# Three-pass products for the block-diagonal gates and the attention-weighted sums of a two-block transformer kernel

## The chip, the cores and the metric

The kernel runs on one core of one Trainium2 chip, as one program. A core has TensorE (PE, the matmul array), VectorE (DVE), ScalarE (ACT), GpSimd (POOL), a queue that issues loads (SyncE, SP), the on-chip memory SBUF (128 partitions) and PSUM, into which TensorE writes its products. The metric is device time in microseconds for one execution; the time of a kernel is the median of its runs.

## What is computed

A sequence of 512 tokens of width 1024 in float32 passes a first block (which this change does not touch) and then two equal layers of a second block. Cut to what matters, a layer is:

```
x = x + 0.5 * swiglu(rms_norm(x, ffn1_norm), w_gate, w_up, w_down)      # width 2816
h = rms_norm(x, mix_norm)
q, k, v, f_logit, xr, gr, g_attn, g_rnn = split(h @ w_in + b_in)
q, k = rms_norm per head; 8 heads of 128
y_attn = forgetting_attention(q, k, v, log_sigmoid(f_logit)) @ w_o_attn
xr = causal_depthwise_conv(xr)                                          # 4 taps
yr = rg_lru(xr) * gelu(gr);  y_rnn = yr @ w_o_rnn
x = x + (sigmoid(g_attn) * y_attn + sigmoid(g_rnn) * y_rnn) @ w_out
x = x + 0.5 * swiglu(rms_norm(x, ffn2_norm), ...)

forgetting_attention, a head, a block of 128 queries:
    s = q_i @ k.T * scale + (c_i[:, None] - c[None, :])    # c = cumsum(log_f)
    p = softmax(where(causal, s, -inf));   out = p @ v
rg_lru:
    r, i = sigmoid(block_diag(x, w_a) + b_a), sigmoid(block_diag(x, w_x) + b_x)   # 16 blocks of 64 x 64
    a = exp(-8 r softplus(-lam));  h_t = a_t h_(t-1) + sqrt(1 - a_t^2) i_t x_t
```

## The kernel before, in words

Activations lie transposed in SBUF, as tiles of 128 channels by 512 tokens. Every large product is made in three passes: each factor is split into a `hi` and a `lo` half (`split`, L222; `w`, L183, for weights), and `mm3` (L228) issues hi x hi, hi x lo and lo x hi (L230, L231, L232) with fp32r operands into one accumulator. Weights come from HBM in chunks of 256 KB in a planned order; for each chunk ScalarE makes `hi` (L198), VectorE makes `lo` (L199), and a ring of four holds each of raw, hi and lo. `acc` gives the four PSUM accumulators (tag `a`); `pair` makes two output tiles of 128 channels, `tokens` makes four tiles of 128 tokens by 512 columns. Four more PSUM banks are named `xm` (1), `xh` (1) and `xs` (2).

SBUF tiles come from pools by tag, each tag with so many buffers: an allocation beyond them waits for the oldest reader to be done. Pools opened inside an `ExitStack` give their memory back at its end, and the next pool opened takes that memory. The order of the instructions on each engine is laid out when the program is built, by a scheduler that takes, of what is ready by its own clock, the earliest in the program's text first, and work under `hp()` before other work. On the chip each engine then keeps that order.

In a layer's mixer (`mix`, L966) the order in the text is: the sum of squares to a scale per token (`stats`), four pairs for `xr`, the recurrent branch (`rnn`, L899), the forget gates (L1014 to L1032, whose cumulative row goes through DRAM and comes back as `cb`, one row a head, spread over the partitions), and then twice, for four heads each (`hf` 0 and 1): tokens for q, k and v with their eviction at L1044, the normalising and transposing of q and k (`heads_T`, L379, which runs under `hp()`; four transposes at L400 through the one bank `xm`, each copied to SBUF at L402), `attn`, and two pairs for the gelu branch. Then come the two output projections with their gates, and `w_out`.

In `rnn` each of the eight channel tiles is convolved (L910, L912), and the two gates are plain f32 matmuls with 128 x 128 block-diagonal weights (L914, L915). In `attn` each head has four query blocks: `attn_scores` (L841) makes the scores and the softmax, one row of tiles `s`; `attn_values` (L861) transposes the weights block by block (L868), copies them to SBUF (L870) and multiplies v with them as plain f32 matmuls of 128 columns (L872), one block behind the scores. The sums of a head gather in `xh` and are copied to a tile `x` (L886). v has six tiles of its own, `qk` five, `cb` two, `bq` (the bias row of q, k or v) one; `keep`, which lives through the whole kernel, has `x` (8), `y` (1) and `p` (1) among others.

Of the kernel before, what the change touches and what calls it, by code (L numbers as in the profile page):

```python
# [7 lines left out]
F32 = mybir.dt.float32  # L8
F32R = mybir.dt.float32r
U8 = mybir.dt.uint8  # L10
AF = mybir.ActivationFunctionType
OP = mybir.AluOpType
# [107 lines left out]
class Build:  # L120
# [98 lines left out]
        self.tc.keep_in_program_order(ins)  # L219
        return ins  # L220

    def split(self, src, tag):  # L222
        hi, lo = self.t(tag, F32R), self.t(tag, F32R)
        self.nc.scalar.copy(hi, src)
        self.nc.vector.tensor_tensor(lo, src, hi.bitcast(F32), op=OP.subtract)
        return hi, lo
# [631 lines left out]
        nc.vector.tensor_scalar(s, s, ri, None, op0=OP.mult)  # L858
        return st

    def attn_values(self, st, v, vc, i, o):  # L861

        nc = self.nc
        n = (i + 1) * 128
        pt = self.aux("xs")
        for j in range(i + 1):
            js = slice(j * 128, j * 128 + 128)
            nc.tensor.transpose(pt[:, js], st[:, js], self.ident)  # L868
        pT = self.t("pT")
        nc.scalar.copy(pT[:, :n], pt[:, :n])  # L870
        for j in range(i + 1):
            nc.tensor.matmul(o[:, i * 128:n], v[j][:, vc:vc + 128], pT[:, j * 128:j * 128 + 128],  # L872
                             start=(i == 0 and j == 0), stop=(i == 3 and j == 3), skip_group_check=True)

    def attn(self, qT, kT, v, hd0, ct, cdram):

        nc = self.nc
        out, todo = [], []

        def values(st, hd, i):  # L880
            if i == 0:
                out.append(self.aux("xh"))
            self.attn_values(st, v, (hd - hd0) * 128, i, out[-1])
            if i == 3:
                y = self.t("x")
                nc.scalar.copy(y, out[-1])  # L886
                out[-1] = y

        for hd in range(hd0, hd0 + 4):
            cb = self.t("cb")  # L890
            nc.gpsimd.dma_start(cb, cdram[hd:hd + 1, :].to_broadcast([128, 512]))
            for i in range(4):
                todo.append((self.attn_scores(qT[hd - hd0], kT[hd - hd0], i, hd, ct, cb), hd, i))
                if len(todo) > 1:
                    values(*todo.pop(0))
        values(*todo.pop(0))
        return out

    def rnn(self, xr, bd, l, hb, sp4):  # L899
        nc = self.nc  # L900
        hs = []
        for j0 in range(0, 8, 4):
            av, vv, ix = [], [], []
            for j in range(j0, j0 + 4):
                xc = self.t("xc")
                for tap in range(CW2):
                    wv = self.col(("conv_w_2", l), j * CW2 + tap)
                    src = xr[j][:, tap:tap + 512]
                    if tap == 0:
                        nc.vector.tensor_scalar(xc, src, wv, self.col(("conv_b_2", l), j), op0=OP.mult, op1=OP.add)  # L910
                    else:
                        nc.vector.scalar_tensor_tensor(xc, src, wv, xc, op0=OP.mult, op1=OP.add)  # L912
                ga, gx = self.aux("xs"), self.aux("xs")
                nc.tensor.matmul(ga, bd[0][j // 4][:, j % 4], xc, start=True, stop=True)  # L914
                nc.tensor.matmul(gx, bd[1][j // 4][:, j % 4], xc, start=True, stop=True)  # L915
                ti, th, a = self.t("abc"), self.t("abc"), self.t("hm")
                nc.scalar.activation(th, ga, AF.Tanh, scale=0.5, bias=hb[:, j:j + 1])
                nc.scalar.activation(ti, gx, AF.Tanh, scale=0.5, bias=hb[:, 8 + j:9 + j])
                nc.scalar.activation(a, th, AF.Exp, scale=sp4[:, 8 + j:9 + j], bias=sp4[:, 8 + j:9 + j])
                nc.scalar.activation(th, th, AF.Tanh, scale=sp4[:, j:j + 1], bias=sp4[:, j:j + 1])  # L920
                a2 = self.square(a, "xc")
                nc.vector.scalar_tensor_tensor(th, a2, 1.0, th, op0=OP.add, op1=OP.mult)
                nc.vector.scalar_tensor_tensor(ti, ti, 1.0, xc, op0=OP.add, op1=OP.mult)
                av.append(a)
                vv.append(th)
                ix.append(ti)
            for v in vv:
                self.pin(nc.scalar.activation(v, v, AF.Sqrt, scale=0.25))
            for a, v, i in zip(av, vv, ix):
                nc.vector.tensor_tensor(i, i, v, op=OP.mult)  # L930
                nc.vector.tensor_tensor_scan(a, a, i, 0.0, op0=OP.mult, op1=OP.add)
            hs += av
        return hs
# [32 lines left out]
    def mix(self, l):  # L966
        nc = self.nc
        h = self.hx
        with ExitStack() as ctx:
            lp = ctx.enter_context(self.tc.tile_pool(name=f"lp{l}", bufs=1))  # L970
            self.pool(ctx, f"mb{l}", hm=8, t=3, bq=1, qk=5, v=6, qkT=8, cb=2, s=3, pT=2)
            with self.hp():
                rt, rb = self.stats()
            hb = self.lined(lp, (128, 32), name="hb")
# [7 lines left out]
            def scaled(a, tag):  # L982
                y = self.t(tag)
                with self.hp():
                    nc.vector.tensor_tensor(y, a, rb, op=OP.mult)
                return y

            ct = self.lined(lp, (128, 32), name="ct")
            cdram = self.dp.tile([8, 512], F32, name=f"cd{l}")
            with ExitStack() as c2:  # L990
                pool = self.pool(c2, f"rn{l}", bd=4, xc=3, abc=8)
                bd = []
                for nm in ("lru_w_a_2", "lru_w_x_2"):
                    b = [self.t("bd", shape=(128, 4, 128)) for _ in range(2)]
                    for hh in range(2):
                        nc.gpsimd.memset(b[hh], 0.0)
                        src = self.ap[nm][l, hh * 8:hh * 8 + 8].rearrange("(j two) c d -> two c j d", two=2)
                        nc.gpsimd.dma_start(b[hh][0:64, :, 0:64], src[0])
                        nc.gpsimd.dma_start(b[hh][64:128, :, 64:128], src[1])
                    bd.append(b)  # L1000

                xr = []
                for m in range(0, 8, 2):
                    for a in self.pair("w_in_2", l, 8, MIX + m * 128, h):
                        y = scaled(a, "t")
                        u = self.lined(pool, (128, 512 + CW2 - 1), tag="xr", bufs=3, name=self.id("xr"))
                        nc.gpsimd.memset(u[:, :CW2 - 1], 0.0)
                        with self.hp():
                            nc.scalar.activation(u[:, CW2 - 1:], y, AF.Identity, bias=self.col(("b_mix", l), len(xr)))
                        xr.append(u)  # L1010
                hs = self.rnn(xr, bd, l, hb, sp4)
                self.tap(f"hs{l}", hs[0])

            fa = self.acc()  # L1014
            for k0 in (0, 4):
                hi, lo = self.w("w_in_2", l, k0, 4, 3072, 128)
# [14 lines left out]
                nc.tensor.transpose(ps[:, i * 8:i * 8 + 8], fc[:, i * 128:i * 128 + 128], self.ident[0:8, 0:8])  # L1031
            nc.vector.tensor_copy(ct, ps[:, 0:32])  # L1032
            self.tap(f"fc{l}", fc)
            ya = []
            for hf in range(2):
                for n in range(3):
                    bq = self.t("bq")
                    c = n * 1024 + hf * 512
                    nc.gpsimd.dma_start(bq, self.ap["brow"][l:l + 1, c:c + 512].to_broadcast([128, 512]))
                    ts = []  # L1040
                    for tt, a in enumerate(self.tokens("w_in_2", l, c, h)):
                        v = self.t("v" if n == 2 else "qk")
                        with self.hp():
                            nc.vector.scalar_tensor_tensor(v, a, rt[:, tt:tt + 1], bq, op0=OP.mult, op1=OP.add)  # L1044
                        ts.append(v)
                    if n == 0:
                        qT = self.heads_T(ts, 4, 128, qg)
                    elif n == 1:
                        kT = self.heads_T(ts, 4, 128, self.col(("k_norm_2", l)))
# [19 lines left out]
            for n, (o, wn) in enumerate(((3072, "w_o_rnn_2"), (2048, "w_o_attn_2"))):  # L1069
# [4 lines left out]
                for m in range(0, 8, 2):  # L1074
                    ga = self.pair("w_in_2", l, 8, MIX + o + m * 128, h)
                    yo = self.pair(wn, l, 8, m * 128, yh if n else yr)
                    for i in range(2):
                        with self.hp():
                            s = scaled(ga[i], "t" if n else "hm")
# [3 lines left out]
                            if n:  # L1083
                                g = mg[m + i]
# [6 lines left out]
            x = self.x  # L1091
# [100 lines left out]
```

## Time and profile before

| | us |
|---|---|
| median of 3 runs | 3413.01 (3413.0 to 3414.46) |
| the profiled execution | 3414.17 |
| its span, first to last instruction | 3412.4 |
| PE busy | 3390.8 |
| DVE busy | 1877.1 |
| ACT busy | 1307.6 |
| POOL busy | 165.0 |

The trace names an instruction by engine, line of the kernel, operation, and the tiles it writes and reads (out<-in). Matmuls are pipelined: their durations overlap, so what one of them occupies on TensorE is read from the distance between starts. A plain f32 matmul is recorded as two matmuls; a transpose, and a pass of `mm3`, as one. The records' starts just after a plain f32 matmul can lie early by the time that the matmul ahead still takes.

### The profile page before, as it was taken

To read this page: it belongs to the slowest core of one execution; us is meant where nothing else is said; L and a number is where in the kernel's file an instruction comes from. 1 tells how busy PE (TensorE), PEld (TensorE's weight loads), DVE (VectorE), ACT (ScalarE), POOL (GpSimd) and SP (SyncE) were. 2 spreads that over 40 slices of the span, in tenths; PEclk is the share of its full clock that TensorE was granted. 3 is DMA by queue.
4 is the path that set the end of the run, shared out by engine and by line. 5 is a ranking of instruction groups with operands and counts; after the bars stand their busy time and mean duration, and the time that the engine had idled before them with its cause. 6 is when DMAs were issued, how large, how long until landed. Compare 5 with 4: busy or idle time off the path is not lost.

```text
span 3412.4 us, 41999 instructions
## 1 busy us (share of the span) xinstructions
PE 3390.8 (99%) x15370; PEld 2769.3 (81%) x15370; DVE 1877.1 (55%) x3148; ACT 1307.6 (38%) x2282; POOL 165.0 (5%) x274
## 2 busy tenths in 40 slices
PE   8999999999999999999999999999999999999999
PEld 6887777888888888788888888888887788888887
DVE  7698654534444444876455444444447865454442
ACT  3335443423333333654333333333336544343331
POOL 0011100000000001111000000000010110000000
PEclk9999999999999999999999999999999999999999
DMA  6223533433333333322333333333343222333332
GB/s 217 72 76 105 155 113 108 130 98 97 96 96 96 96 117 105 90 91 89 111 97 95 99 96 97 95 99 96 102 123 95 86 89 81 123 95 98 96 104 91
DMA packets 180623, 351.33 MB, mean 103 GB/s; under 512 B 20672, under 2 KB 21952, under 8 KB 180416
## 3 DMA queue, kind: packets, MB, share of 16 engines
q1 hardware_dynamic: 174112, 329.07, 31.8%
q0 software_dynamic: 6160, 19.37, 1.8%
q8 instruction: 121, 1.98, 0.2%
q14 instruction: 86, 0.70, 0.1%
q10 hardware_dynamic: 144, 0.20, 0.0%
HBM read 342.24 MB, written 6.32 MB: 102 GB/s over the span
## 4 chain that ended last, share of the span: by engine, by line
PE 97%; DVE 2%; ACT 1%; issue 0%; DMA 0%; POOL 0%; SPq 0%; DVEq 0%; ACTq 0%
PE a L232 30%; PE a L230 30%; PE a L231 30%; PE xh L872 1%; PE xs L847 1%; PE xh L437 1%; PE xh L519 1%; PE xs L497 1%; PE xs L868 1%; PE xm L400 0%; DVE xc L912 0%; DVE lo L199 0%; PE xh L513 0%; PE xh L476 0%; PE xs L914 0%
## 5 line engine op out<-in xcount | busy, mean ns | idle before, releaser
L199 DVE TENSOR_TENSOR lo<-raw,hi 128x512 fp32r<-128x512 f32 x1144 | 784.8, 687 | 1257.1 <-ACT hi L198 1240.9
L198 ACT CAST hi<-raw 128x512 fp32r<-128x512 f32 x1144 | 707.0, 619 | 1572.2 <-PE a L231 1265.3
L231 PE MATMUL a<-h,hi 128*128 128x512 f32 x2528 | 989.4, 392 | 0.0
L230 PE MATMUL a<-h,hi 128*128 128x512 f32 x2528 | 984.7, 392 | 1.7 <-ACT h L599 1.7
L232 PE MATMUL a<-h,lo 128*128 128x512 f32 x2528 | 982.4, 392 | 0.0
L230 PEld LDWEIGHTS a<-h,hi 128*128 128x128 f32 x2528 | 475.4, 188 | 105.6 <-issue 6.1
L232 PEld LDWEIGHTS a<-h,lo 128*128 128x128 f32 x2528 | 475.1, 188 | 105.2 <-issue 7.2
L231 PEld LDWEIGHTS a<-h,hi 128*128 128x128 f32 x2528 | 475.0, 188 | 101.5 <-issue 3.6
L230 PE MATMUL a<-act,hi 128*128 128x512 f32 x960 | 373.4, 389 | 0.0
L231 PE MATMUL a<-act,hi 128*128 128x512 f32 x960 | 373.4, 389 | 0.0
L232 PE MATMUL a<-act,lo 128*128 128x512 f32 x960 | 372.8, 389 | 0.0
L231 PE MATMUL a<-Y,hi 128*128 128x512 f32 x544 | 214.5, 394 | 0.0
L230 PE MATMUL a<-Y,hi 128*128 128x512 f32 x544 | 213.7, 393 | 0.0
L232 PE MATMUL a<-Y,lo 128*128 128x512 f32 x544 | 212.8, 391 | 0.0
L232 PEld LDWEIGHTS a<-act,lo 128*128 128x128 f32 x960 | 180.2, 188 | 37.5
L230 PEld LDWEIGHTS a<-act,hi 128*128 128x128 f32 x960 | 180.2, 188 | 37.4
L231 PEld LDWEIGHTS a<-act,hi 128*128 128x128 f32 x960 | 180.2, 188 | 37.3
L232 PE MATMUL a<-hi,h 128*128 128x512 f32 x512 | 204.5, 403 | 0.0
L231 PE MATMUL a<-lo,h 128*128 128x512 f32 x512 | 203.7, 398 | 0.0
L230 PE MATMUL a<-hi,h 128*128 128x512 f32 x512 | 199.2, 407 | 1.7 <-DVE qk L1044 1.7
L232 PEld LDWEIGHTS a<-Y,lo 128*128 128x128 f32 x544 | 102.2, 188 | 23.5 <-issue 2.1
L231 PEld LDWEIGHTS a<-Y,hi 128*128 128x128 f32 x544 | 102.2, 188 | 23.1 <-issue 2.0
(294 smaller groups left out, 3042.6 us busy)
## 6 DMA issues: line engine op xcount, KB each, us to landing
raw<-in_w_l SPq DMA_DIRECT2D x852, 256.0 KB, 2.6
raw<-in_w_first SPq DMA_DIRECT2D x284, 256.0 KB, 2.6
mr<-in_mod_b_ SPq DMA_DIRECT2D x32, 513.0 KB, 3.7
mq<-in_mod_a SPq DMA_DIRECT2D x8, 1026.0 KB, 8.0
xs<-x POOLq DMA_DIRECT2D x16, 256.0 KB, 2.3
cb<-cd POOLq DMA_DIRECT2D x16, 256.0 KB, 3.5
x<-xs POOLq DMA_DIRECT2D x16, 256.0 KB, 3.9
bq<-in_brow POOLq DMA_DIRECT2D x12, 256.0 KB, 3.7
```

The costliest lines, as they stand in the source:

```text
L198: nc.scalar.copy(hi, raw)
L199: nc.vector.tensor_tensor(lo, raw, hi.bitcast(F32), op=OP.subtract)
L230: mm(acc, w[0], x[0], start=start, stop=False)
L231: mm(acc, w[0], x[1], start=False, stop=False)
L232: mm(acc, w[1], x[0], start=False, stop=stop)
L437: mm(ps[:, i * 64:i * 64 + 64], k[:, s], q[:, s].rearrange("p (n c h) -> p n c h", c=2, h=h)[:, :, 1], start=True, stop=True)
L497: mm(z[:, o:o + n], q[pr, blk(i)], k[pr, :n], start=True, stop=True)
L519: mm(pt[pr, c], v[j][:, hd * 64:hd * 64 + 64], f[:, o + j * 128:o + j * 128 + 128], start=j == 0, stop=j == i, skip_group_check=True)
L847: nc.tensor.matmul(ps[:, :n], qT[:, ts], kT[:, :n], start=True, stop=True)
L868: nc.tensor.transpose(pt[:, js], st[:, js], self.ident)
L872: nc.tensor.matmul(o[:, i * 128:n], v[j][:, vc:vc + 128], pT[:, j * 128:j * 128 + 128], start=(i == 0 and j == 0), stop=(i == 3 and j == 3 ...
```

## The change

The gates of the recurrent branch and the attention-weighted sums are made with `mm3` instead of with plain f32 matmuls. For the gates the block-diagonal weights are staged in tiles of the tag `abc` and split into `bd` (now eight tiles), and the convolved channel tile is split into two tiles `x` before it is multiplied. For the sums v is evicted into `qk` and split into `v` (eight tiles, in a pool of their own, `at`, opened after the recurrent branch has given its memory back); the sums of a head are made together, by blocks of keys instead of blocks of queries: for block j the transposed weights of all later queries are gathered (512 - 128 j columns), split into hi and lo, and multiplied in three passes. They follow after the second score block of the next head. `s` has five tiles instead of three. The row `cb` alternates between its one tile and the tile `p` of `keep`, and `bq` takes the tile `y` of `keep`.

```diff
-    def split(self, src, tag):
-        hi, lo = self.t(tag, F32R), self.t(tag, F32R)
+    def split(self, src, tag, shape=(128, 512)):
+        hi, lo = self.t(tag, F32R, shape), self.t(tag, F32R, shape)
...
-    def attn_values(self, st, v, vc, i, o):
+    def attn_values(self, sts, v, vc):
         nc = self.nc
-        n = (i + 1) * 128
-        pt = self.aux("xs")
-        for j in range(i + 1):
+        o = self.aux("xh")
+        for j in range(4):
             js = slice(j * 128, j * 128 + 128)
-            nc.tensor.transpose(pt[:, js], st[:, js], self.ident)
-        pT = self.t("pT")
-        nc.scalar.copy(pT[:, :n], pt[:, :n])
-        for j in range(i + 1):
-            nc.tensor.matmul(o[:, i * 128:n], v[j][:, vc:vc + 128], pT[:, j * 128:j * 128 + 128],
-                             start=(i == 0 and j == 0), stop=(i == 3 and j == 3), skip_group_check=True)
+            n = 512 - j * 128
+            pt = self.aux("xs")
+            for i in range(j, 4):
+                nc.tensor.transpose(pt[:, (i - j) * 128:(i - j) * 128 + 128], sts[i][:, js], self.ident)
+            hi, lo = self.t("pT", F32R), self.t("pT", F32R)
+            nc.scalar.copy(hi[:, :n], pt[:, :n])
+            nc.vector.tensor_tensor(lo[:, :n], pt[:, :n], hi[:, :n].bitcast(F32), op=OP.subtract)
+            self.mm3(o[:, j * 128:], [a[:, vc:vc + 128] for a in v[j]], (hi[:, :n], lo[:, :n]), j == 0, j == 3)
+        y = self.t("x")
+        nc.scalar.copy(y, o)
+        return y
...
         for hd in range(hd0, hd0 + 4):
-            cb = self.t("cb")
+            cb = self.t("cb" if hd % 2 else "p")
             nc.gpsimd.dma_start(cb, cdram[hd:hd + 1, :].to_broadcast([128, 512]))
+            sts = []
             for i in range(4):
-                todo.append((self.attn_scores(qT[hd - hd0], kT[hd - hd0], i, hd, ct, cb), hd, i))
-                if len(todo) > 1:
-                    values(*todo.pop(0))
-        values(*todo.pop(0))
+                sts.append(self.attn_scores(qT[hd - hd0], kT[hd - hd0], i, hd, ct, cb))
+                if i == 1 and todo:
+                    out.append(self.attn_values(*todo.pop(0)))
+            todo.append((sts, v, (hd - hd0) * 128))
+        out.append(self.attn_values(*todo.pop(0)))
...
-                nc.tensor.matmul(ga, bd[0][j // 4][:, j % 4], xc, start=True, stop=True)
-                nc.tensor.matmul(gx, bd[1][j // 4][:, j % 4], xc, start=True, stop=True)
+                xd = self.split(xc, "x")
+                for g, b in ((ga, bd[0][j // 4]), (gx, bd[1][j // 4])):
+                    self.mm3(g, [v[:, j % 4] for v in b], xd, True, True)
...
-            self.pool(ctx, f"mb{l}", hm=8, t=3, bq=1, qk=5, v=6, qkT=8, cb=2, s=3, pT=2)
+            self.pool(ctx, f"mb{l}", hm=8, t=3, qk=5, qkT=8, cb=1, s=5, pT=2)
...
-                pool = self.pool(c2, f"rn{l}", bd=4, xc=3, abc=8)
+                pool = self.pool(c2, f"rn{l}", bd=8, xc=3, abc=8)
...
-                    b = [self.t("bd", shape=(128, 4, 128)) for _ in range(2)]
+                    b = [self.t("abc", shape=(128, 4, 128)) for _ in range(2)]
...
-                    bd.append(b)
+                    bd.append([self.split(v, "bd", (128, 4, 128)) for v in b])
...
+            self.pool(ctx, f"at{l}", v=8)
             ya = []
             for hf in range(2):
                 for n in range(3):
-                    bq = self.t("bq")
+                    bq = self.t("y")
...
                     for tt, a in enumerate(self.tokens("w_in_2", l, c, h)):
-                        v = self.t("v" if n == 2 else "qk")
+                        v = self.t("qk")
                         with self.hp():
                             nc.vector.scalar_tensor_tensor(v, a, rt[:, tt:tt + 1], bq, op0=OP.mult, op1=OP.add)
-                        ts.append(v)
+                            ts.append(self.split(v, "v") if n == 2 else v)
```

## Rows read from the trace of the kernel before

**Rows 1.** The page: busy shares (part 1), granted clock by slices (2), chain (4).
```profile
PE 3390.8 (99%) x15370; PEld 2769.3 (81%) x15370; DVE 1877.1 (55%) x3148; ACT 1307.6 (38%) x2282; POOL 165.0 (5%) x274
...
PEclk9999999999999999999999999999999999999999
...
PE 97%; DVE 2%; ACT 1%; issue 0%; DMA 0%; POOL 0%; SPq 0%; DVEq 0%; ACTq 0%
```

**Rows 2.** Timeline of PE at the first gate: start, duration, instruction, how many.
```profile
1339.76 0.39 PE L231 MATMUL a<-h,hi 128*128 128x512 f32 x1
...
1349.74 1.02 PE L914 MATMUL xs<-xc,bd 128*128 128x512 f32 x2
1350.59 1.02 PE L915 MATMUL xs<-xc,bd 128*128 128x512 f32 x2
...
1351.68 0.40 PE L231 MATMUL a<-h,hi 128*128 128x512 f32 x1
```

**Rows 3.** Timeline of PE, plain products of 128 columns in attention.
```profile
1466.09 0.60 PE L872 MATMUL xh<-pT,v 128*128 128x128 f32 x4
1466.53 0.49 PE L868 MATMUL xs<-cst,s 128*128 128x128 f32 x3
```

**Rows 4.** Timeline of PE, plain products of 64 columns in the first block.
```profile
106.98 1.00 PE L437 MATMUL xh<-qs,kf 128*128 128x64 f32 x8
...
108.11 0.39 PE L231 MATMUL a<-h,hi 128*128 128x512 f32 x1
```

**Rows 5.** Groups of PE by form: count, busy us, mean ns, idle before.
```profile
L872 PE MATMUL xh<-pT,v 128*128 128x128 f32 x320 | 46.2, 274 | 0.0
...
L914 PE MATMUL xs<-xc,bd 128*128 128x512 f32 x32 | 16.3, 591 | 0.0
```

**Rows 6.** Timeline of PE between the q and the k tokens, first layer.
```profile
1413.71 0.40 PE L232 MATMUL a<-hi,h 128*128 128x512 f32 x1
1414.48 0.66 PE L400 MATMUL xm<-cst,qk 128*128 128x128 f32 x4 [0.38 <-ACT qkT L402]
1415.99 0.50 PE L230 MATMUL a<-hi,h 128*128 128x512 f32 x1 [0.86 <-DVE qk L1044]
```

**Rows 7.** Timeline of PE where the v tokens end, first and second half.
```profile
1439.42 0.39 PE L232 MATMUL a<-hi,h 128*128 128x512 f32 x1
1439.65 0.40 PE L230 MATMUL a<-h,hi 128*128 128x512 f32 x1
...
1553.27 0.39 PE L232 MATMUL a<-hi,h 128*128 128x512 f32 x1
...
1554.15 0.60 PE L400 MATMUL xm<-cst,qk 128*128 128x128 f32 x4
```

**Rows 8.** Timeline of ACT: copies after k's transposes, first half.
```profile
1430.38 0.69 ACT L402 ACTIVATE qkT<-xm,cv 128x512 f32<-128x512 f32 x1 [0.74 <-PE xm L400]
...
1436.06 0.69 ACT L402 ACTIVATE qkT<-xm,cv 128x512 f32<-128x512 f32 x1 [0.50 <-PE xm L400]
...
1444.88 0.67 ACT L402 ACTIVATE qkT<-xm,cv 128x512 f32<-128x512 f32 x1
...
1449.69 0.68 ACT L402 ACTIVATE qkT<-xm,cv 128x512 f32<-128x512 f32 x1
```

**Rows 9.** Groups of DVE by form: a split's `lo`; an eviction of v.
```profile
L225 DVE TENSOR_TENSOR Y<-x,Y 128x512 fp32r<-128x512 f32 x24 | 16.6, 692 | 5.3 <-PE a L231 5.1
...
L1044 DVE SCALAR_TENSOR_TENSOR v<-a,m,bq 128x512 f32<-128x512 f32 x16 | 11.3, 746 | 7.2 <-PE a L232 7.2
```

**Rows 10.** Timeline of ACT: attention's last output, and its first reading.
```profile
1653.28 0.58 ACT L886 COPY x<-xh 128x512 f32<-128x512 f32 x1
...
1676.40 0.62 ACT L224 CAST Y<-x 128x512 fp32r<-128x512 f32 x1 [0.36 <-PE a L231]
```

**Rows 11.** Windows: length, busy us of PE, PEld, DVE, ACT, POOL, clock, DMA.
```profile
1380.00:1420.00 40.00, 38.77 (x167) 29.50 (x166) 37.51 (x59) 28.63 (x45) 4.28 (x5) 1.00 0.28 84
```

**Rows 12.** Timeline of POOL: the first bias row's load.
```profile
1307.13 0.54 POOL L1039 DMA_DIRECT2D bq<-in_brow  x1
```

More of the change, by code (lines that the diff above doesn't have):

```diff
@@ L878, in attn @@
         out, todo = [], []
[L880 to L887, printed above, removed]
         for hd in range(hd0, hd0 + 4):
-            cb = self.t("cb")
+            cb = self.t("cb" if hd % 2 else "p")
             nc.gpsimd.dma_start(cb, cdram[hd:hd + 1, :].to_broadcast([128, 512]))
+            sts = []
             for i in range(4):
-                todo.append((self.attn_scores(qT[hd - hd0], kT[hd - hd0], i, hd, ct, cb), hd, i))
-                if len(todo) > 1:
-                    values(*todo.pop(0))
-        values(*todo.pop(0))
+                sts.append(self.attn_scores(qT[hd - hd0], kT[hd - hd0], i, hd, ct, cb))
[3 more added lines that the diff above has]
+        out.append(self.attn_values(*todo.pop(0)))
         return out
```

## The prediction, made before the change was run

> **What bounds the kernel now.** I read the page's busy shares and the chain first. TensorE is busy for 3390.8 of 3412.4 us, it is 97% of the chain that ended last, and its clock is granted in full in every slice [rows 1]. So the time is the sum of what each matmul occupies on TensorE, and any other engine counts only where TensorE waits for it. The change touches only the mixer of the two layers of the second block, so I went there next.
>
> The second view is the TensorE timeline, read by starts, because the durations in it overlap. From the start at 1339.76 to the one at 1349.74 lie 44 starts of three-pass matmuls of 512 columns: 9.98 / 44 = 0.227 us each [rows 2]. A plain f32 product appears as two records. The four records of L914 and L915 run from 1349.74 to 1351.45 (the L231 at 1351.68 less the 0.227 of the L230 before it), so one record occupies 1.71 / 4 = 0.428 us, one product 0.856 us [rows 2]. At 128 columns four records occupy 1466.53 - 1466.09 = 0.44 us, 0.11 each [rows 3]. At 64 columns eight occupy 108.11 - 0.227 - 106.98 = 0.90 us, again 0.11 each [rows 4]: half the columns, the same time, so a matmul that loads its own weights does not go below 0.11 here.
>
> The third view is where TensorE waits inside the mixer: in one place per layer, between the q tokens and the k tokens. I come to it below, since the change makes another place of that kind.
>
> **Gates of the recurrent branch.** Removed: 32 products, that is 64 records (32 of L914 [rows 5] and, two for two beside them, 32 of L915 [rows 2]), 64 x 0.428 = 27.4 us. Added: 96 passes of 512 columns, 96 x 0.227 = 21.8 us. TensorE gains 5.6 us, and there is little to dispute in it: the added passes are the commonest instruction of the kernel.
>
> **Attention-weighted sums.** Removed: 320 records of 128 columns [rows 5], 320 x 0.11 = 35.2 us. The 160 transposes stay. Added: for each of 16 heads four blocks of three passes, with 512, 384, 256 and 128 columns. The trace has no three-pass matmul below 512 columns. From below, the cost in proportion to columns is 3 x 0.227 x 1280/512 = 1.70 us a head, 27.2 us. From above, every pass costs the 0.227 of 512 columns: 12 x 0.227 = 2.72, 43.6 us. I take the proportion down to the floor of 0.11, since the 128- and 64-column records are the nearest rows: 3 x (0.227 + 0.170 + 0.114 + 0.11) = 1.86 us a head, 29.8 us. Gain 5.4 us; bounds from a gain of 8.0 to a loss of 8.4.
>
> Here a rule can be weighed against the rows. The Trainium skill, "FP8 and Floating Point Precision", section "TensorE Precision Notes", counts a true FP32 product as four passes through the array. Three of four would be a quarter saved in both parts: 8.8 + 6.9 = 15.7 us. The rows say otherwise: 0.227 for a pass, but 0.856 / 4 = 0.214 for a quarter of a product, and a floor at 128 columns. By the rows it is 5.6 + 5.4 = 11.0 us.
>
> **The new wait: v passes through the `qk` tiles.** Before, v was evicted from PSUM into six tiles of its own; now it goes into `qk`, which has five, and is split from there. Four of the five hold k until the last of its four transposes (L400). The second to fourth evictions of v therefore wait for those transposes; behind them stand the four accumulators and the next pair of products (the gelu branch), which has one free accumulator for 6 x 0.227 = 1.4 us and then needs a second. The same happens now between q and k, and shows the price: the last L400 starts at 1414.48 instead of 1413.94, and the next product at 1415.99 instead of 1414.92, because L1044 had no tile; together 1.6 us [rows 6]. For v in the first half: its last matmul starts at 1439.42 and the next product at 1439.65 [rows 7], while the copies that follow k's four transposes start at 1430.38, 1436.06, 1444.88 and 1449.69 [rows 8]. If the last two steps are drawn forward when TensorE has nothing else, the wait is that of q and k, or nothing; if they stay where they are, it is 1449.7 + 0.75 for the eviction [rows 9] - 1441.0 = 9.4 us. In the second half v ends at 1553.27 and k's last transposes stand at 1554.15 [rows 7], with scores of other heads around them, so 0 to 1.6. I take 1.6 for each first half, the nearest row, and 0.8 for each second half: 2 x 2.4 = 4.8 us; bounds 0 and 18.8 + 3.2. On VectorE, which is in order, the `lo` halves of streamed weights stand behind a waiting eviction, and TensorE's next chunk behind those; the price above includes that, as it does between q and k.
>
> **What lies beside TensorE.** Splits of four weight tiles, eight conv outputs and eight v tiles a layer are 20 x 0.69 on VectorE [rows 9] and 20 x 0.62 on ScalarE [rows 10]: 13.8 and 12.4 us. The `lo` of the transposed weights adds at most 2.5 x 0.75 = 1.9 us a head on VectorE (1280 columns read from PSUM, as the eviction reads 512) [rows 9], 15 us a layer; the ScalarE copy was there before. VectorE is nearly full in places, 37.5 of 40 us between 1380 and 1420, and of TensorE's 40 only the waits between q and k were lost there [rows 11]; so the extra 29 us a layer become lateness of the recurrent branch and of attention. What covers that: attention's last output is written at 1653.28 and first read at 1676.40 [rows 10], 23 us in hand. I cost it at nothing; beyond 23 us it would cost TensorE microsecond for microsecond. The split of v also waits for memory of the recurrent branch, and in the second half for the first half's last sums; only the score-weighted sums stand behind it, inside the same 23 us.
>
> Five score tiles for one head of four let the next head run ahead by one block, and `cb` alternating with `p` keeps two rows in flight: nothing. `bq` now takes the tile `y` and waits for the last normalised split of the layer before; its first issue was at 1307.13 on GpSimd [rows 12], with the loads of the gate weights queued behind it, and nothing reads those before 1349.74 [rows 2]. Nothing, unless it is over 35 us late.
>
> **The sum.** 5.6 + 5.4 - 4.8 = 6.2 us off. The profiled execution took 3414.17 us (span 3412.4 and 1.8 around it): 3408.0. The median of the runs, 3413.01, lies 1.2 below the profiled one: 3406.8 us.
>
> **Rivals.** (a) The waits on `qk` vanish, since TensorE has scores and gate products to fill in: 11.0 off, 3402.0. For it: after k in the second half no wait is seen. Against: q and k in both first halves. (b) A pass costs a quarter of the plain product that it stands for: (35.2 + 27.4) / 4 = 15.7, less 4.8, 3402.1. Against it stand the two prices [rows 2]; only the shorter passes could still come near it. That is the count of the Trainium skill's page weighed above. (c) A pass of 128 columns costs two records, 0.22, as every plain product of that width does: the sums give 3 x (0.227 + 0.170 + 0.114 + 0.22) x 16 = 35.1 us, no gain, so 0.9 off in all, 3412.1. The change then does only half of what it says. (d) Slower: every pass costs 0.227 whatever its columns, because something other than streaming sets it. The sums lose 8.4, in all 7.6 longer, 3420.6. For it: 0.227 is above the 0.214 that streaming explains. Against: nothing in the rows ties it to a fixed time. It turns the sign when the mean pass of the sums exceeds (35.2 + 5.6 - 4.8) / 192 = 0.188 us. (e) Slower: v's evictions wait for the transposes where they now stand, 9.4 us in each first half: 18.8 - 11.0, 3420.8; it decides from 5.5 us a layer on. Against it: the transposes are marked urgent.
>
> **How the numbers follow.** About 0.2%, 6.8 us, is what a measurement can tell here from no change: faster is below 3406.2, slower above 3419.8. Forecast 0.42, (a) 0.15, (b) 0.08, (c) 0.17, (d) 0.08, (e) 0.10. The forecast lies just inside no change, and a third of it falls below the line. Faster: (a), (b) and 0.14 of the forecast, 0.37. Slower: most of (d) and (e) with larger waits, 0.13. Within: 0.50. The range, 3401.0 to 3419.0, takes in (a), (b) and (c) and stops short of (d) and (e).
>
> **What would show it.** Right: no rows of two records at the gates and the sums; L230 to L232 at 0.227 on gate tiles; 0.17, 0.11 and 0.11 between starts for 384, 256 and 128 columns; waits of TensorE on `qk` L1044 of 1 to 2 us after v. Wrong: 0.22 or more at 128 columns (c, d); no wait after v (a); a wait of 5 us or more (e); or TensorE waiting for weights or for attention's outputs, which I cost at nothing.

## The result: slower by 0.83%, and the profile after

| | before | after |
|---|---|---|
| median | 3413.74 us (3413.0 to 3414.57, 4 runs) | 3442.11 us (3440.9 to 3442.7, 4 runs) |
| ratio | | 1.0083 [1.0071, 1.0094] |
| profiled execution, its span | 3414.17, 3412.4 | 3440.9, 3439.1 |

The forecast was 3406.8, with a range of 3401.0 to 3419.0; the kernel came out at 3442.1, 28.4 us slower than before, above the range and by causes that no rival named. Of the signs that the prediction listed for being wrong, one came: TensorE waits for attention's outputs. The page of the changed kernel, against [rows 1]:

```profile
PE 3394.3 (99%) x15274; PEld 2767.5 (80%) x15274; DVE 1927.4 (56%) x3252; ACT 1326.8 (39%) x2322; POOL 165.4 (5%) x274
...
PEclk9999999999999999999999999999999999999999
...
PE 96%; DVE 2%; ACT 1%; issue 0%; DMA 0%; POOL 0%; SPq 0%; DVEq 0%; ACTq 0%
```

Read alone, the page would mislead: TensorE is 99% busy, and its busy time even rose by 3.5 us, though it has 96 records fewer. What is new stands in the table of waits (engine, line, what it waited for, us in all, times, longest):

```profile
PE xs L847 <- DVE s L850: 10.1, 6, 3.0
PE a L230 <- DVE t L982: 6.9, 4, 3.1
...
PE a L230 <- ACT Y L224: 2.6, 2, 1.3
PE a L230 <- DVE qk L1042: 2.6, 2, 1.3
```

Only the last of these is the wait of [rows 6], 1.7 us before. The first three were not there. L847 makes the scores, L982 scales the gelu branch's accumulators, and this L224 splits attention's outputs for their projection.

A wait shows only what TensorE stood still for; what a thin stretch costs is more. So I took, from TensorE's records in the first of the two layers, the distance from the end of each matmul to the end of the next, less what the later one occupies (0.227 us for a three-pass matmul of 512 columns, 0.43 for a record of a plain product of 512, in proportion below that, a plain record not under 0.11), and summed what is over by more than 0.06. I call it **time lost**. It is 1.9 us in the kernel before and 20.2 in the kernel after: 3.5 before 1425 us, 12.2 from 1425 to 1500, 0.4 to 1650, 4.0 to 1800. The second layer repeats it. So 2 x 18.3 = 36.6 us were lost, the cheaper products saved 12.2 (below), and the difference, 24.4, is most of the span's 26.7. Of the other 2.3, some 1.9 lie in distances that are over by less than 0.06 us each.

**The prices.** Timeline of TensorE in attention: start, duration, instruction.

```profile
1713.71 0.22 PE L230 MATMUL xh<-pT,v 128*128 128x128 f32 x1
1713.77 0.28 PE L231 MATMUL xh<-pT,v 128*128 128x128 f32 x1
1713.88 0.27 PE L232 MATMUL xh<-pT,v 128*128 128x128 f32 x1
1713.99 1.07 PE L847 MATMUL xs<-qkT,qkT 128*128 128x512 f32 x2
...
1728.51 0.34 PE L230 MATMUL xh<-pT,v 128*128 128x384 f32 x1
1728.68 0.34 PE L231 MATMUL xh<-pT,v 128*128 128x384 f32 x1
1728.86 0.34 PE L232 MATMUL xh<-pT,v 128*128 128x384 f32 x1
1729.03 0.27 PE L870 MATMUL xs<-cst,s 128*128 128x128 f32 x1
```

From start to start, 384 columns take 0.17 us. Of the three passes of 128 columns, which stand in a row here behind one of 512, the first takes 0.06 and the other two 0.11 each, 0.28 together. Over the trace, from the end of the matmul before to a pass's own end, the 24 passes of 128 columns that stand behind any other matmul take 0.057 to 0.062 us; the 20 that stand directly behind another pass of 128 columns, with no wait between, take 0.110 to 0.114. Ten of the sixteen triples have other work behind their first pass, so that a triple costs 0.25 on average. It is 0.227 to 0.231 for 512 columns, 0.171 to 0.176 for 384, 0.115 to 0.119 for 256. The gates cost 96 x 0.227 = 21.8 us and the sums 29.0; the plain products took 27.4 and 35.6, 63.0 together, so 12.2 was saved where I had 11.0.

**The first loss, at 1470 to 1486.** The same timeline between the last matmul of a full stretch and the next one:

```profile
1470.42 0.91 PE L847 MATMUL xs<-qkT,qkT 128*128 128x384 f32 x2
1474.30 1.12 PE L847 MATMUL xs<-qkT,qkT 128*128 128x512 f32 x2 [2.96 <-DVE s L850]
1476.13 0.80 PE L847 MATMUL xs<-qkT,qkT 128*128 128x128 f32 x2 [0.71 <-DVE s L850]
1478.29 1.22 PE L847 MATMUL xs<-qkT,qkT 128*128 128x256 f32 x2 [1.36 <-DVE s L850]
1479.30 0.42 PE L870 MATMUL xs<-cst,s 128*128 128x128 f32 x1
1482.75 0.79 PE L230 MATMUL a<-hi,h 128*128 128x512 f32 x1 [3.03 <-DVE t L982]
```

VectorE in that stretch is full, and more than half of it is not attention's (of the 13 us from 1470 to 1483 the scans and the products before them take 6.9, the splits of v and `Y` 3.4, attention 5.0, with some overlap):

```profile
1472.05 1.21 DVE L928 TENSOR_TENSOR_SCAN hm<-hm,abc 128x512 f32<-128x512 f32 x1
1473.18 0.66 DVE L927 TENSOR_TENSOR abc<-abc,abc 128x512 f32<-128x512 f32 x1
1473.77 0.47 DVE L850 SCALAR_TENSOR_TENSOR s<-xs,ct,p 128x256 f32<-128x256 f32 x1
...
1476.00 1.21 DVE L928 TENSOR_TENSOR_SCAN hm<-hm,abc 128x512 f32<-128x512 f32 x1
...
1478.61 0.68 DVE L225 TENSOR_TENSOR v<-qk,v 128x512 fp32r<-128x512 f32 x1
1479.21 0.77 DVE L225 TENSOR_TENSOR Y<-t,Y 128x512 fp32r<-128x512 f32 x1
```

The scores' eviction, L850, stands among them in VectorE's order. L928 is the last step of the recurrent branch. Its last scan stands at 1476.00; before, at 1450.8. Behind it come the splits of v and of the gelu branch (`Y`), whose tiles lie in the memory that the branch gives back. The gelu branch's three tiles `t` stay full until then, so its next scaling, L982, comes at 1482.02, and TensorE's next chunk of products at 1482.75. The recurrent branch, which stands in no term of the forecast, is 25 us late.

**Why it is late.** The first of the two gate activations of its eight tiles (ScalarE; count, durations in ns, start of the first and of the last), before and then after:

```profile
L917 ACT ACTIVATE abc<-xs,hb x8: 669/687/689, 1350.8 to 1437.6; 128x512 f32<-128x512 f32 x8
```

```profile
L914 ACT ACTIVATE abc<-xs,hb x8: 672/690/690, 1350.5 to 1463.0; 128x512 f32<-128x512 f32 x8
```

Both begin at the same time. The first seven come 12.1 us apart before ((1423.3 - 1350.8) / 6) and 15.3 after ((1442.2 - 1350.5) / 6). One tile after, on VectorE:

```profile
1415.59 0.54 DVE L906 TENSOR_SCALAR xc<-xr,cv 128x512 f32<-128x512 f32 x1
...
1419.87 0.75 DVE L908 SCALAR_TENSOR_TENSOR xc<-xr,cv,xc 128x512 f32<-128x512 f32 x1
...
1422.22 0.69 DVE L225 TENSOR_TENSOR x<-xc,x 128x512 fp32r<-128x512 f32 x1
...
1429.89 0.54 DVE L906 TENSOR_SCALAR xc<-xr,cv 128x512 f32<-128x512 f32 x1
```

and on ScalarE:

```profile
1421.48 0.61 ACT L224 CAST x<-xc 128x512 fp32r<-128x512 f32 x1
...
1427.98 0.69 ACT L914 ACTIVATE abc<-xs,hb 128x512 f32<-128x512 f32 x1 [2.32 <-PE xs L232]
...
1431.07 0.63 ACT L312 ACTIVATE xc<-hm 128x512 f32<-128x512 f32 x1
```

The convolution ends at 1420.6, and its `lo` at 1422.9: the split has put 2.3 us between the convolution and the gates. Over the last seven tiles, from the end of the convolution to the gate activation it is 7.8 us on average, against 4.4 before; these 3.4 are about what a tile takes longer. The next tile's convolution (L906) does not begin before the gates of this one are through. The work is one chain of eight links, and the change has made each link longer. The code says why it could be a chain: the square `a2` (L312) takes its tile from the same tag `xc` as the convolution, and tiles of one tag are handed out in the order of the text, so that the next convolution gets its tile only after this tile's square has got one.

**The second loss, at 1729 to 1735.** Attention's last output and its first reading, on ScalarE, against [rows 10]:

```profile
1731.48 0.59 ACT L876 COPY x<-xh 128x512 f32<-128x512 f32 x1 [0.85 <-PE xh L232]
...
1732.10 0.62 ACT L224 CAST Y<-x 128x512 fp32r<-128x512 f32 x1
```

In the kernel before, the eight outputs were split one after another; the first of these splits is the 1676.40 of [rows 10], and the last output's own is the eighth:

```profile
1685.77 0.62 ACT L224 CAST Y<-x 128x512 fp32r<-128x512 f32 x1
```

The last output is written 78.2 us later than before, and TensorE's first matmul with it waits (1.32 us, 1732.77). The 78 us have two parts. The first output of the eight comes at 1516.4 instead of 1479.4, 37.0 late, of which 25.8 is the late start (the first score at 1468.0 instead of 1442.1); and from the first to the last it is 215.1 us instead of 173.9, so 30.7 instead of 24.8 us a head.

### The profile page after: what moved, and what is told of

The parts are those of the page before. It is cut to its first block, busy times and chain, and to the rows that moved or that the text cites. A ratio compares the mean times of both kernels' runs of the same rounds, so it can differ in the third digit from the quotient of the medians.

```text
span 3439.1 us, 41933 instructions
## 1 busy us (share of the span) xinstructions
PE 3394.3 (99%) x15274; PEld 2767.5 (80%) x15274; DVE 1927.4 (56%) x3252; ACT 1326.8 (39%) x2322; POOL 165.4 (5%) x274
## 4 chain that ended last, share of the span: by engine, by line
PE 96%; DVE 2%; ACT 1%; issue 0%; DMA 0%; POOL 0%; SPq 0%; DVEq 0%; ACTq 0%
PE a L230 30%; PE a L232 30%; PE a L231 30%; PE xs L847 1%; PE xh L437 1%; PE xh L519 1%; PE xs L497 1%; PE xs L870 0%; DVE hm L928 0%; PE xh L231 0%; PE xh L230 0%; PE xm L400 0%; DVE abc L927 0%; PE xh L232 0%; PE xh L513 0%
## 5 line engine op out<-in xcount | busy, mean ns | idle before, releaser
L230 PEld LDWEIGHTS a<-hi,h 128*128 128x128 f32 x512 | 96.4, 190 | 30.8 <-DVE t L982 7.4
```

What stands on the lines that cost most here:

```text
L230: mm(acc, w[0], x[0], start=start, stop=False)
```

## Theories and experiments

Three causes were on the table; the expectations, written one after the other, call them by letters. **Chain** (C): the split lies inside the serial chain of the recurrent branch; everything that shares the branch's memory and banks comes late. **One pair** (P; A in the first expectations, where it is only attention's new order): the sums of a head take the two tiles `pT` as one hi/lo pair, so block after block waits for the pair, and attention overruns. **Wait on `qk`** (Q; V in the first expectations, together with the wait for memory): the term of the forecast, v's eviction behind k's transposes. The rival to the chain: fuller VectorE and ScalarE, wherever the work stands.

**Only the chain, with nothing else of the change.** The kernel before with two more instructions a tile between convolution and gates: a copy, and the maximum of the tile and its copy.

```diff
-                nc.tensor.matmul(ga, bd[0][j // 4][:, j % 4], xc, start=True, stop=True)
-                nc.tensor.matmul(gx, bd[1][j // 4][:, j % 4], xc, start=True, stop=True)
+                xd, xe = self.t("x"), self.t("x")
+                nc.scalar.copy(xd, xc)
+                nc.vector.tensor_tensor(xe, xc, xd, op=OP.max)
+                nc.tensor.matmul(ga, bd[0][j // 4][:, j % 4], xe, start=True, stop=True)
+                nc.tensor.matmul(gx, bd[1][j // 4][:, j % 4], xe, start=True, stop=True)
```

> The kernel before with plain products throughout, but with a ScalarE copy and a VectorE maximum of 512 columns between the convolved tile and its gates, so that the chain of a tile is as long as with the split; no pass, tile of v or order of attention is changed. Theory C: the branch ends near 1476 us and TensorE waits about 10 us a layer more: 3425 to 3440 us. Theories V and A: 3413 to 3415 us.

3436.28 us, 1.0063 [1.0048, 1.0078] of the kernel before in the same comparison (3414.53): 21.7 us longer, though TensorE has the same work. The gate activations (L920 there), and TensorE at the place of the first loss:

```profile
L920 ACT ACTIVATE abc<-xs,hb x8: 687/687/689, 1350.0 to 1465.9; 128x512 f32<-128x512 f32 x8
```

```profile
1470.66 0.81 PE L847 MATMUL xs<-qkT,qkT 128*128 128x128 f32 x4
1479.72 0.48 PE L868 MATMUL xs<-cst,s 128*128 128x128 f32 x1 [8.24 <-DVE s L858]
```

It is the same place: 13.8 us are lost a layer, 11.0 of them from 1425 to 1500, and nothing at attention's end (last output 1667.3). A tile takes 16.3 us here. This run has more work on the two engines as well as a longer chain; the run that parts these follows below. 1.3 us of work a tile on two engines that are 55% and 38% busy costs more than the whole change was to bring.

**Plain gates in the kernel after.** The sums and v's new path stay; the gates' weights go back to four plain tiles.

```diff
-                xd = self.split(xc, "x")
-                for g, b in ((ga, bd[0][j // 4]), (gx, bd[1][j // 4])):
-                    self.mm3(g, [v[:, j % 4] for v in b], xd, True, True)
+                nc.tensor.matmul(ga, bd[0][j // 4][:, j % 4], xc, start=True, stop=True)
+                nc.tensor.matmul(gx, bd[1][j // 4][:, j % 4], xc, start=True, stop=True)
...
```

> The changed kernel with the gates of the recurrent branch made as before (plain f32 products from the convolved tile, four weight tiles, no split); the attention part stays as changed. Theory C (chain): the split of the convolved tile stands in a chain that runs tile by tile and makes each of the eight tiles 3 us longer, the branch ends 25 us late, and TensorE, which has then nothing but work that needs the branch's result or its memory, waits some 12 us a layer. By C the branch ends near 1452 us again, the waits of TensorE between 1470 and 1483 us are gone, and the time is 3405 to 3415 us. Theory V (v and the Y tiles wait for qk tiles and for memory, which the attention part brought): the waits stay, 3440 us or more, since the gates' cheaper passes are lost too. Theory A (attention is slower by its new order and ends too late for the output projection): part of the waits stay, those before the attention projection, 3415 to 3425 us.

3424.21 us, 1.0027 [1.0016, 1.0038]: above what the chain alone would give, and in the range of A. The last gate activation is back at 1436.2 and the waits at 1470 are gone; 9.5 us a layer are still lost, 3.2 at 1446 to 1450 and 4.3 at attention's end (last output 1721.4). So there is a second cause in the sums alone.

**One more `xc`.** Is it the number of tiles?

```diff
-                pool = self.pool(c2, f"rn{l}", bd=8, xc=3, abc=8)
+                pool = self.pool(c2, f"rn{l}", bd=8, xc=4, abc=8)
```

> The changed kernel with four tiles xc instead of three. Theory C in its closer form: tiles of a tag are handed out in the order of the text, so the convolution of tile j+1 waits until the square of tile j has taken up its tile, however many there are; then a tile still takes 15 us, the branch still ends near 1476 us, and the time is 3438 to 3444 us. If the ring is merely too short, the branch ends at least 10 us earlier and the time falls below 3432 us.

3444.23 us, 1.0087 [1.0072, 1.0102], no better than after.

```profile
L914 ACT ACTIVATE abc<-xs,hb x8: 670/688/689, 1350.2 to 1462.6; 128x512 f32<-128x512 f32 x8
```

**The square in another tag.** Or is it that both take turns in one tag?

```diff
-                a2 = self.square(a, "xc")
+                a2 = self.square(a, "x")
```

> The changed kernel with the square of the decay in a tile x: now the split of tile j+1 waits for the square of tile j, but its convolution no longer does. Theory C: a tile takes 12 to 13 us instead of 15, as in the kernel before, the branch ends between 1450 and 1460 us, and the 12 us a layer at its end mostly go; the waits before the attention projection stay (4 us a layer): 3416 to 3426 us. If the chain is not the cause, 3440 us.

3420.65 us, 1.0018 [1.0008, 1.0027]: 21.5 of the 28.4 us are back, by one word.

```profile
L914 ACT ACTIVATE abc<-xs,hb x8: 683/690/691, 1350.5 to 1432.1; 128x512 f32<-128x512 f32 x8
```

```profile
1425.00:1500.00 75.00, 72.27 (x323) 57.83 (x322) 60.76 (x117) 41.37 (x78) 8.05 (x14) 0.98 0.30 92
```

(Window: length, busy us of PE, PEld, DVE, ACT, POOL, granted clock, DMA.) In after TensorE is busy for 66.59 of these 75 us. With the split in place and the chain broken, the last activation comes earlier than in the kernel before (1437.6). The extra work on VectorE is the same, so the rival, fuller engines, falls: VectorE is busy for 60.76 us of this window here and for 60.57 in after. A tile takes 11.7 us. 5.0 us remain at 1444 to 1451 and 3.2 at attention's end, where the last output is still written at 1721.0.

**A second pair for the sums**, from the eight tiles `x`, in every other block, where those are free (the first six heads).

```diff
...
-            hi, lo = self.t("pT", F32R), self.t("pT", F32R)
+            tag = "x" if j % 2 and free else "pT"
+            hi, lo = self.t(tag, F32R), self.t(tag, F32R)
...
-            todo.append((sts, v, (hd - hd0) * 128))
+            todo.append((sts, v, (hd - hd0) * 128, hd < 6))
```

> The changed kernel with the hi and lo of the transposed weights in two pairs of tiles instead of one (odd blocks take free tiles x, for the first six heads). Theory P (one pair): in the change the sums of a head go block after block because hi and lo of a block fill both tiles pT until its three passes are done; a head takes 30 us instead of 24, and attention ends at 1731 us, after the output projection wanted it. By P a head takes 22 to 26 us here, the last output is written before 1700 us, the 4 us a layer before the attention projection go, and the 12 us a layer at the end of the recurrent branch stay: 3430 to 3436 us. If not P, attention ends at 1725 us or later and the time stays at 3440 us or more.

3432.89 us, 1.0054 [1.0039, 1.0069]. The last output is written at 1707.19, 24.3 us earlier, a little after the 1700 that I had written down, and in the window where TensorE is busy for 47.86 us in after, it is now busy for all 50:

```profile
1700.00:1750.00 50.00, 50.00 (x225) 41.46 (x224) 22.35 (x34) 16.58 (x27) 0.54 (x1) 1.00 0.35 101
```

The loss at 1425 to 1500 is unchanged, 12.2. The two causes are separate. But a head still takes 28.9 us ((1707.2 - 1504.8) / 7), not the 22 to 26 that I had written down: the pair is not all that makes attention slower.

**Both.**

> The changed kernel with both: the square in x and two pairs of tiles for hi and lo. If C and P together account for what was lost (12 and 4 us a layer, with a few us for the waits on qk): 3401 to 3414 us, the kernel before or better. If something else is lost as well, above 3418 us.

3411.8 us, 0.9992 [0.9983, 1.0002]. The last output is written at 1680.5 and nothing is lost behind it. What is left is at one place, on TensorE and then on VectorE:

```profile
1444.04 0.49 PE L847 MATMUL xs<-qkT,qkT 128*128 128x128 f32 x2 [1.25 <-DVE s L850]
1446.01 0.83 PE L847 MATMUL xs<-qkT,qkT 128*128 128x256 f32 x2 [1.48 <-DVE s L850]
```

```profile
1445.94 2.06 DVE L1043 SCALAR_TENSOR_TENSOR qk<-a,m,y 128x512 f32<-128x512 f32 x3
```

TensorE's rows name the scores' eviction there. I read it as v: three of its four evictions stand together at 1445.94, and the first at 1432.08. By this it is the wait of the forecast, at 5.0 us a layer, and the next run tests it. Not all of the 5.0 is standing still: from 1446.5 to 1449.9 the granted clock is 0.51, and seven passes of 512 columns take 3.15 us instead of 1.59.

**v of the first half in the tiles `x`, on top of both.**

```diff
-                        v = self.t("qk")
+                        v = self.t("x" if n == 2 and hf == 0 else "qk")
```

> The kernel with both repairs (the square in x, two pairs of tiles for hi and lo), and v of the first half evicted into free tiles x instead of qk, so that its second to fourth evictions no longer wait for the last transposes of k. Theory Q (the wait on qk that the prediction priced at 1.6 us a layer): with the two other causes gone, what is left between 1444 and 1450 us, some 5 us a layer, is this wait; it goes, and the time is 3399 to 3405 us, below the kernel before. If the wait is that of the scores on VectorE at the end of the recurrent branch instead, it stays: 3409 to 3413 us.

3402.06 us, 0.9962 [0.9949, 0.9976]: 12.9 us faster than the kernel before. 1.6 us a layer are lost, as before the change (1.9), and TensorE is full at the place of the first loss:

```profile
1425.00:1500.00 75.00, 75.00 (x350) 60.96 (x349) 64.50 (x130) 44.92 (x87) 12.36 (x15) 1.00 0.31 95
```

**The same edit on the kernel after, alone.**

> The changed kernel with that one difference: v of the first half evicted into tiles x. By theories C and P the wait on qk is hardly seen in the changed kernel, because TensorE then runs out of work on the recurrent branch anyway: 3438 to 3442 us, as the changed kernel. If the wait on qk was what cost it the time, it falls below 3430 us.

3434.56 us, 1.0058 [1.0044, 1.0071], 3.4 below the lower end: a miss. The last gate activation came at 1447.6 instead of 1463.0, with 7.8 us lost at 1425 to 1500 instead of 12.2, and 6.1 at attention's end instead of 4.0. I had taken the wait on `qk` as hidden under the chain; the run shows that it also held the chain up. The way I read out of the trace is VectorE, on which a waiting eviction stands ahead of the branch's last tiles; no run tests that by itself.

**The sums alone**, that is plain gates, two pairs and v in `x`.

> The changed kernel with the gates as before (plain products, no split), two pairs of tiles for hi and lo, and v of the first half in tiles x: the attention-weighted sums alone, with the waits that they brought taken out. If the passes cost what the trace of the changed kernel shows (0.23, 0.17, 0.12, and 0.06 to 0.11 for 512, 384, 256 and 128 columns), the sums save 6 to 7 us and the time is 3405 to 3410 us; with the gates' 5.6 us on top that is the 3402 us of the kernel with all repairs. If the two parts disturb each other otherwise, it lies above 3412 us.

3410.25 us, 0.9990 [0.9981, 0.9999], 0.25 above the range. The sums save 3.9 us and the gates on top of them about 9, where the prices say 6.6 and 5.6. The interval of the first runs from 0.3 to 6.5 us, so 6.6 lies just outside, though this trace loses hardly more than the kernel before by the measure above; where the 2.7 went I did not place. Only the sum of some 12.9 is firm.

**Freeing the branch entirely.** Three kernels asked whether the chain could be opened further: after and before with the square in a tile of its own (`sq`), and before with the square in `x`.

```diff
-                a2 = self.square(a, "xc")
+                a2 = self.square(a)
```

> The changed kernel with one difference: the square of the decay (a2) takes its tile from sq instead of from the ring xc, so that the next tile's convolution no longer has to wait until the square of this one has been taken up. Theory C: the eight tiles overlap, the branch ends before 1455 us in spite of the split, the waits of 12 us a layer go, and the cheaper products show: 3398 to 3412 us. Theories V and A: no change beyond 5 us, 3437 to 3442 us.

> The kernel before with the same difference (a2 in sq). Theory C: the branch ends earlier than 1452 us, but TensorE did not wait for its end, so little comes of it: 3408 to 3414 us (at most the 1.7 us a layer between q and k). Theories V and A say nothing of it: 3413 us.

> The kernel before with the square of the decay in a tile x. By theory C the branch ends some 5 us earlier than 1452 us, but TensorE did not wait for its end there: 3409 to 3415 us. If it gains more than 4 us, part of what the repaired kernels win has nothing to do with the change.

All three missed on the same side: 3430.47 us, 1.0045 [1.0028, 1.0062]; 3426.27, 1.0034 [1.0021, 1.0047]; 3427.2, 1.0039 [1.0025, 1.0052]. The branch is early (last gate activation at 1413.0 in the first of them), and time is lost elsewhere: 11.3, 6.4 and 7.6 us a layer before 1425. The waits of the first, and the third at one such place, on TensorE and on VectorE:

```profile
PE a L230 <- DVE qk L1042: 15.3, 6, 4.4
```

```profile
1393.23 1.10 PE L914 MATMUL xs<-xc,bd 128*128 128x512 f32 x2 [2.01 <-DVE xc L912]
```

```profile
1393.00 0.75 DVE L1044 SCALAR_TENSOR_TENSOR qk<-a,m,bq 128x512 f32<-128x512 f32 x1
```

I read it so: gates are put into TensorE's fixed order before their convolution is done, and convolutions and scans stand on VectorE ahead of the evictions of q. q is evicted at 1393.0 in the third and at 1393.2 in the second, against 1381.0 before. That reading was not tested by a run of its own. What the runs do show: the edit that gives 21.5 us in the kernel after costs 12.3 in the kernel before, so the 12.9 us of the best kernel are not owed to it alone.

## Why the prediction was wrong, step by step

**Gates, -5.6: right.** 0.227 us a pass and 21.8 us, as forecast.

**Sums, -5.4: right, and a little too careful.** 29.0 us against 29.8, so -6.6 with the 35.6 that the plain ones took. The floor of 0.11 at 128 columns [rows 3, rows 4] holds for passes directly behind one another too; what I had not seen is that a pass behind another matmul takes 0.06, and half of the passes of 128 columns stand so. So rivals (c) and (d), 0.22 and 0.227 at 128 columns, fall with the timeline above, and no sign turns there. Of the rule of the Trainium skill, "FP8 and Floating Point Precision", section "TensorE Precision Notes" (a true FP32 product counts as four passes), three quarters of the plain products' 63.0 us would be 47.3, as an estimate; the trace has 50.8. That is rival (b), and the measurement decides against it, by 3.5 us.

**The wait on `qk`, +4.8: the mechanism right, the term mis-sized, and hidden.** In the kernel after hardly anything is lost there (0.6 us at 1443.6); TensorE stood at the chain's end soon after. With the chain broken it costs 5.0 us a layer at the first half's v, where I took 1.6 with a bound of 9.4. Rival (a), that it vanishes, was wrong by that; rival (e), the full 9.4, was not what happened either. The edit that removes it is worth 9.7 us in the end (3411.8 to 3402.06).

**"I cost it at nothing": the step that failed.** The paragraph on what lies beside TensorE summed the added work an engine, 13.8 and 12.4 and 15 us, turned it into "lateness of the recurrent branch and of attention", and compared that with 23 us in hand at attention's end. Three things were wrong in it.

- It counted busy time where it had to count the length of a chain. Eight conv splits are 8 x 1.3 = 10.4 us of work; as links of a serial chain they cost 25 us, because each also queues on two engines in order (2.3 us from the end of the convolution to the end of the split in the tile shown, and 15.3 against 12.1 us a tile). The chain alone, on the kernel before, cost 21.7 us.
- It named one reader of the late work, the projection of attention. The branch's end had nearer ones: scores, v's splits and the gelu branch's, all of which wait for its memory or stand behind its scans. There was less in hand there than the branch came late: before, the scores began at 1442.1, with the branch's last scan at 1450.8; in the run with the longer chain that scan comes 27.1 us later, and 10.9 us a layer are lost.
- Attention's lateness was 78.2 us and not 29, against the 23 in hand. The two tiles `pT`, which held two blocks in flight before, stand nowhere in the forecast; one block now takes both. The 23 us themselves were a misreading: 1676.40 is the split of the first output, the last is split at 1685.8, so 32.5 us were in hand. And beyond them the price was not microsecond for microsecond: 45.7 us beyond cost 4.0 us a layer, since TensorE had other products in its order (busy for 47.86 us between 1700 and 1750). With the chain broken, the second pair alone brings the last output from 1721.0 to 1680.5; with the chain left as it is, it is still 1707.2; and the chain alone, on the kernel before, leaves it at 1667.3, in time. So most of the second loss is the pair's, and the chain adds to it. Even the best kernel needs 28.6 us a head ((1676.8 - 1476.6) / 7); what sets that I did not look into, since it is in time.

The sum of the three repairs, one at a time on the kernel after, is 21.5 (square) + 9.2 (pairs) + 7.5 (v) = 38.2 us; together they give 40.0. So the changed products were worth a little more than the forecast said, and three times as much was lost around them. The range missed because it was built from the terms that had rows; the term at nothing had no bound above the 23 us.

## What to carry to other kernels

An engine at 99% does not mean that work beside it is free: what it does next was settled when its queue was laid out, and a chain off the critical path that feeds this queue counts by its length, link by link, not by its engines' busy time. Before costing an added instruction at nothing, find the loop that it stands in, ask whether the loop's rounds can overlap (which tiles they take, under which tag, and in which order these are handed out), and multiply by the rounds. And when one buffer becomes a pair, halve the number of blocks in flight.

## What the runs showed of the hardware

Two things that I had not expected. A three-pass matmul of 128 columns takes 0.06 us behind another matmul and 0.11, as a plain record of the same width, directly behind a pass of 128 columns: three in a row take 0.28 us (1713.71 to 1713.99 above), three with other work behind the first 0.23. And short waits cost more than their length: windows of the kernel after, around the first loss (columns as above, the clock is the third number from the end):

```profile
1470.00:1474.00 4.00, 1.34 (x4) 0.30 (x3) 4.00 (x7) 1.63 (x2) 1.13 (x1) 1.00 0.00 0
1474.00:1478.00 4.00, 1.92 (x4) 0.80 (x4) 4.00 (x8) 1.20 (x4) 2.49 (x2) 0.68 0.00 0
1478.00:1482.00 4.00, 1.43 (x3) 0.73 (x3) 4.00 (x10) 4.00 (x10) 2.06 (x4) 0.50 0.21 66
1482.00:1486.00 4.00, 3.25 (x8) 2.61 (x9) 4.00 (x10) 1.24 (x4) 0.25 (x1) 0.54 0.00 0
1486.00:1490.00 4.00, 4.00 (x21) 3.23 (x20) 4.00 (x12) 3.38 (x11) 0.00 (x0) 1.00 0.41 134
```

While TensorE is busy for 1.3 to 1.9 of 4 us, the granted clock falls from 2.4 to 1.2 GHz (0.50), and it is still there when the work is back at 1482.75, so that passes of 512 columns take 0.43 to 0.59 us from start to start instead of 0.227. The seven that start from 1482.75 to 1485.48 take 3.04 us instead of 1.59; that much of the 12.2 us, at least, is the clock. The page's row of the clock, in slices of 86 us, shows nothing of it.
